# Expert rows stored unnormalised, gathered whole, turned on TensorE, and scattered by row

## The chip, the cores and the metric

The kernel runs on one core of a Trainium2 chip. The time is device microseconds (us) of one execution. Engines: PE (TensorE matmul; PEld is its weight load), DVE (VectorE), ACT (ScalarE), POOL (GpSimd), SP (SyncE). SP, ACT and POOL issue DMAs, each on a queue of its own (q1, q10, q0 in the profile), served by 16 DMA engines.

## What is computed

Two transformer blocks over 512 tokens with 1024 features (D), in float32. The change lies in the last part of the second block, a mixture of 32 experts of which each token takes two from one group:

```
def hierarchical_moe(h, w_rg, b_rg, w_re, b_re, w_gate, w_up, w_down):
    hf = h.reshape(-1, d)                        # h = rms_norm(x, ffn_norm_g)
    g_prob = softmax(hf @ w_rg + b_rg)           # 4 groups
    g_sel = argmax(g_prob);  g_w = g_prob[g_sel]
    e_in_group = (hf @ w_re + b_re)[g_sel]       # 8 experts of that group
    top_p, top_i = top_k(softmax(e_in_group), 2);  top_p = top_p / sum(top_p)
    combine = one_hot(g_sel * 8 + top_i) * (g_w * top_p)
    for every expert e:
        hid = silu(hf @ w_gate[e]) * (hf @ w_up[e])      # 1024 -> 256
        y += (hid * combine[:, e]) @ w_down[e]           # 256 -> 1024
    return y
```

The result is added to the residual x; a gated per-layer embedding follows (`per_layer`), and then the output is written.

## The kernel before

The residual lives in SBUF as 8 chunks `h[k]` of 128 features x 512 tokens. `mixed` adds the last matmuls of the attention part into it chunk by chunk; `router` (L1766) is interleaved with it: as a chunk is ready, its products with the router's weights (L1789) and its squares (L1794) go to TensorE. `gain` is the identity times the norm's weights.

`route` (L1821) then makes, for 4 blocks of 128 tokens, 64 products with `gain` (L1899), which turn the chunks to rows of tokens and multiply by the norm's weights; ACT copies them with the factor of the rms (`xrow`), and four DMAs of ACT's queue store them in DRAM as `xd`, 512 rows of 4 KB. Beside it DVE computes the choice of experts in an order written by hand (L1903 to 2024): one-hots, and a table by matmul (L1881), which gives `gidx`, the index of the token for every slot. A pair of experts is computed together: 64 slots for each, 128 rows. There are 17 positions (16 pairs, and one for experts that have more than 64 tokens; what exceeds that goes through an `overflow` branch, L2133, not taken here).

For each pair `gather_rows` (L2041) issues four indirect DMAs on POOL's queue; each brings quarter rows of 1 KB to 128 partitions, so that four DVE transposes in blocks of 32x32 (`turn_rows`, L2049; `first_rows`, L2061, for the first pair) give `xe`, features x slots. A slot without a token has an index out of range and moves nothing. Then: `up_products` (L2073) 16 products (the trace has two records for each), with the turn of the pair before (`expert_turn`, L2093) behind the first; ACT's silu and one DVE operation (L2085, `eact`); `expert_down` (L2106) 8 products, also with two records; ACT copies the result to `ys`, and ACT's queue stores all 128 rows into `yd` (512 KB, L1717) for pairs 0 to 13. The last three positions stay in SBUF and are brought to their tokens by products with one-hots (`spread`).

The weights, 6 MB per pair, come in pieces of 1 MB on SP's queue (`run` and the ring, L344) into buffers that products release. So this queue goes on when TensorE has used a buffer.

At the end, `rows_back` (L1745) gathers each token's two rows of `yd` by eight indirect DMAs on POOL's queue; `combine` adds up the spread positions (L1757), adds the two rows of each token on DVE (L1760, the "y adds") and turns them by products with the identity (L1762). Then `per_layer`. A scheduler orders the instructions of each engine outside the part that is written by hand; engines run their instructions in order.

Of the kernel before, what the change touches and what calls it, by code (L numbers as in the profile page):

```python
# [22 lines left out]
P = 128  # L23
T = 512
# [30 lines left out]
NSLOT = NST * P + P  # L55
NGR = 4 * NBL
# [3 lines left out]
def shape_constants():  # L60
# [32 lines left out]
    r[:, 32:64] = 2 * (np.arange(32) % NPR) + np.arange(32) // NPR  # L93
    r[:, 64:72] = np.tile(t[:, None] + P * np.arange(TT) + 1, 2)
    r[:, 72:73] = t[:, None] // 32 - 4
    r[:, 73:74] = t[:, None]
# [47 lines left out]
def layout(I):  # L144
# [57 lines left out]
    gu = gu.reshape(NE, 4, KD, 32, 512).transpose(0, 1, 3, 2, 4).reshape(NE, P, 2, 2048)  # L202
    A["w_eg"] = gu.transpose(0, 2, 1, 3).reshape(2 * NE, P, 2048)
# [187 lines left out]
class Kernel:  # L391
# [144 lines left out]
    def run(self, stop):  # L536
# [27 lines left out]
        self.yd = dp.tile([NSLOT, D], F32, name="yd")  # L564
# [1064 lines left out]
    def experts(self, rp, gain, *logits):  # L1629
# [4 lines left out]
        with ExitStack() as ctx:  # L1634
# [3 lines left out]
            r = dict(  # L1638
                slot=kp.tile([P, 2, TT], I32, name="slot"),
                gidx=kp.tile([P, NGR], I32, name="gidx"),  # L1640
                over=self.over,
                table=kp.tile([P, 2, NBL], F32, name="etable"),
                iota=self.w_rt[:, 0:P],
                rows=self.w_rt[:, P:2 * P].rearrange("p (a n) -> p a n", a=2),
                quarter=kp.tile([P, 1], F32, name="quarter"),
            )
            turns = ExitStack()
            tp = turns.enter_context(self.pool("eturn", side="right"))
            xv = xd.rearrange("t (q c) -> (t q) c", q=4)
            gath = [[gain[:, 2 * i:2 * i + 2].rearrange("p a b -> p (a b)") for i in range(4)]]  # L1650
            xe, hid, turned, pairs, begun = {}, {}, {}, [], []

            def first():
                xe[0] = tp.tile([P, KD, P], F32, name="xe")
                yield from self.first_rows(xe[0], gath[0], r["gidx"][:, 0:4], xv)
                begun.extend(self.up_products(xe[0], ring))
                yield begun[-1][1]
            with ExitStack() as c2:
                self.route(c2, tp, xd, r, first(), gain, *logits)
            with ExitStack() as c2:  # L1660
# [606 lines left out]
```

## Time and profile before

| | us |
|---|---|
| median of three runs | 2211.03 (2206.07 to 2212.96) |
| the profiled execution | 2210.73 |
| its span | 2209.0 |
| PE busy | 2081.9 |
| DVE busy | 1069.6 |
| ACT busy | 788.2 |
| POOL busy | 346.7 |

The shares are averages: PE is busy 94% of the whole span, and the experts' part (about 1812 to 2131 us) has other limits. Rows of the timelines give the start, the length and the count of a group of like instructions, and in brackets how long the engine had been idle and what released it.

### The profile page before, as it was taken

Reading aid. Unit: us, or ns where it says so; the run is one execution under the profiler, and the core shown is the slowest. Engines: PE = TensorE matmul, PEld = TensorE weight load, DVE = VectorE, ACT = ScalarE, POOL = GpSimd, SP = SyncE. Lnnn points to the kernel's source line nnn. Section 1 sums busy time; section 2 is a strip of 40 time slices with the busy share of each in tenths; the row PEclk is TensorE's granted clock in tenths of the full one; section 3 lists DMA queues with packets and bytes.
Section 4 is the critical chain, followed back from the end, with each engine's and each line's share of the span. In section 5 each row is a group of like instructions: output and inputs, shape, how many; then the busy total and the mean of one; then the engine's idle time right before and its main releaser. Section 6 shows DMA issues by size and latency. Waiting matters only on the chain. (4 is left out here: it accounts for less than half of the span.)

```text
span 2209.0 us, 25845 instructions
## 1 busy us (share of the span) xinstructions
PE 2081.9 (94%) x10170; PEld 1616.3 (73%) x10170; DVE 1069.6 (48%) x1973; ACT 788.2 (36%) x1186; POOL 346.7 (16%) x444
## 2 busy tenths in 40 slices
PE   7999999999999999999999999999999995977597
PEld 5677788888889878888788888888878882322166
DVE  7887644344476563554554344446654423101136
ACT  4676433122357432333432222343443221111133
POOL 3222200000113111221200000120111114322113
PEclk9999999999999999999999999999999997999899
DMA  5122322322225200110122222322202466999941
GB/s 179 63 78 77 124 96 96 105 96 95 77 70 182 70 33 15 50 47 20 42 93 99 102 96 96 103 98 96 90 29 96 171 251 228 413 416 417 393 161 39
DMA packets 67588, 281.50 MB, mean 127 GB/s; under 512 B 8784, under 2 KB 10104, under 8 KB 54788
## 3 DMA queue, kind: packets, MB, share of 16 engines
q1 hardware_dynamic: 59300, 260.43, 32.2%
q0 software_dynamic: 4560, 8.94, 1.2%
q10 hardware_dynamic: 3600, 10.41, 1.2%
q8 instruction: 82, 1.34, 0.2%
q14 instruction: 46, 0.38, 0.1%
HBM read 272.40 MB, written 12.06 MB: 129 GB/s over the span
## 5 line engine op out<-in xcount | busy, mean ns | idle before, releaser
L275 ACT ACTIVATE whi<-raw 128x1024 fp32r<-128x1024 f32 (+2 forms) x249 | 261.2, 1054 | 647.4 <-PE bank L420 575.5
L420 PE MATMUL bank<-xh,whi 128*128 128x512 f32 x1160 | 464.2, 400 | 9.2 <-ACT xh L430 7.8
L420 PE MATMUL bank<-xh,wlo 128*128 128x512 f32 x1160 | 458.7, 396 | 14.7 <-DVE wlo L276 14.7
L420 PE MATMUL bank<-xl,whi 128*128 128x512 f32 x1160 | 455.5, 393 | 0.0
L276 DVE TENSOR_TENSOR wlo<-raw,whi 128x1024 fp32r<-128x1024 f32 (+2 forms) x249 | 309.5, 1247 | 191.8 <-ACT whi L275 191.6
L420 PEld LDWEIGHTS bank<-xh,wlo 128*128 128x128 f32 x1160 | 220.1, 190 | 67.4 <-DVE wlo L276 16.9
L420 PEld LDWEIGHTS bank<-xh,whi 128*128 128x128 f32 x1160 | 220.4, 190 | 56.3 <-ACT xh L430 7.8
L420 PEld LDWEIGHTS bank<-xl,whi 128*128 128x128 f32 x1160 | 220.0, 190 | 49.7 <-issue 1.2
L447 POOL TENSOR_TENSOR ssq<-ssq,sq 128x512 f32<-128x512 f32 x27 | 39.2, 1453 | 757.0 <-ACT sq L434 757.0
L2073 PE MATMUL bank<-rawa,xe 128*64 128x512 f32 x328 | 103.5, 662 | 40.1 <-DMA rawa<-w_eg 20.3
L420 PE MATMUL bank<-hidh,whi 128*128 128x512 f32 x352 | 137.1, 389 | 0.0
L420 PE MATMUL bank<-hidh,wlo 128*128 128x512 f32 x352 | 137.0, 389 | 0.0
L420 PE MATMUL bank<-hidl,whi 128*128 128x512 f32 x352 | 137.0, 389 | 0.0
L2073 PEld LDWEIGHTS bank<-rawa,xe 128*64 128x64 f32 x328 | 30.2, 150 | 99.0 <-issue 57.7
L434 ACT ACTIVATE prob<-bank 128x512 f32<-128x512 f32 (+1 forms) x96 | 57.1, 595 | 111.1 <-PE bank L1234 81.3
L818 DVE TENSOR_TENSOR fb<-bank,rows 128x512 f32<-128x512 f32 x44 | 30.4, 691 | 133.2 <-PE bank L420 133.2
L1217 PEld LDWEIGHTS acc<-v,prob 128*128 128x128 f32 x640 | 79.8, 192 | 6.2 <-POOL prob L1244 2.3
L1217 PE MATMUL acc<-v,prob 128*128 128x96 f32 x640 | 82.2, 275 | 1.4 <-POOL prob L1244 1.4
L420 PEld LDWEIGHTS bank<-hidh,wlo 128*128 128x128 f32 x352 | 66.1, 188 | 13.8
L420 PEld LDWEIGHTS bank<-hidl,whi 128*128 128x128 f32 x352 | 66.1, 188 | 13.8
L420 PEld LDWEIGHTS bank<-hidh,whi 128*128 128x128 f32 x352 | 66.1, 188 | 13.7
L815 DVE TENSOR_TENSOR fa<-bank,rows 128x512 f32<-128x512 f32 x44 | 30.4, 690 | 88.5 <-PE bank L420 88.5
(571 smaller groups left out, 3710.7 us busy)
## 6 DMA issues: line engine op xcount, KB each, us to landing
raw<-w_gu SPq DMA_DIRECT2D x44, 1024.0 KB, 4.8
rawa<-w_eg SPq DMA_DIRECT2D x41, 1024.0 KB, 14.2
raw<-w_dn SPq DMA_DIRECT2D x20, 1024.0 KB, 4.8
rawa<-w_ed SPq DMA_DIRECT2D x17, 1024.0 KB, 17.1
raw<-w_eg SPq DMA_DIRECT2D x13, 1024.0 KB, 16.4
raw<-w_mix SPq DMA_DIRECT2D x12, 1024.0 KB, 4.8
rawb<-w_eg SPq DMA_DIRECT2D x9, 1024.0 KB, 17.7
yd<-ys ACTq DMA_DIRECT2D x14, 512.0 KB, 8.2
```

The lines of the kernel that those rows point to most:

```text
L275: nc.scalar.activation(hi, r, AF.Copy)
L276: nc.vector.tensor_tensor(lo, r, hi.bitcast(F32), op=ALU.subtract)
L420: i = nc.tensor.matmul(o, a, b, start=first and n == 0, stop=last and n == N - 1)
L434: return self.nc.scalar.activation(o, i, f, **kw)
L447: self.nc.gpsimd.tensor_tensor(self.ssq, self.ssq, sq, op=ALU.add)
L815: nc.vector.tensor_tensor(a, og, rbc, op=ALU.mult)
L818: nc.vector.tensor_tensor(b, ov, rbc, op=ALU.mult)
L1217: i = nc.tensor.matmul(a[:, h * AW:h * AW + AW], e[:K, h * P:h * P + P], v, start=first and h == 0, stop=last and h == HPG - 1)
L2073: last = nc.tensor.matmul(o[s], xe[:, 4 * pi + k, s], w(k), start=pi == 0 and k == 0, stop=pi == 1 and k == 3)
```

## The change

- `router` has a new step `rows(k)`: as a chunk of the residual is ready, four transposes on TensorE, one ACT copy and one DMA of ACT's queue store its features, raw, into `xd` (256 KB, runs of 512 bytes). The 64 products with `gain` and the ACT copies with the rms are gone; the rms now enters in the silu's factor and in the weight (`table` has a third row of numbers), and the norm's weights are multiplied in as rows are turned.
- `gidx` has two entries for each slot: the token, from which to gather, and the assignment (0 to 1023), to which to scatter. One table of 8 matmuls gives both for the 16 pairs; a second gives the factors; a third (`more`) serves the seventeenth position and the overflow.
- `gather_rows` is one indirect DMA of whole rows of 4 KB. Its two buffers are there from the beginning, and pairs 0 and 1 are fetched at once.
- `turn_rows` is eight transposes on TensorE and two DVE multiplications from PSUM.
- The results of pairs 0 to 13 are scattered by row with an indirect DMA of POOL's queue to `yd`, which now has a row for every assignment and is zeroed wholly (4 MB) at the place where 512 KB were.
- The rows back are four plain DMAs of 1 MB on SP's queue, behind the weights; the y adds are ordered behind the last down product.

```diff
+    A["w_eg"] = gu.reshape(NE, 2, 4, P, 512).transpose(0, 1, 3, 2, 4).reshape(2 * NE, P, 2048)
...
-        self.yd = dp.tile([NSLOT, D], F32, name="yd")
+        self.yd = dp.tile([2 * T, D], F32, name="yd")
...
-            nc.gpsimd.dma_start(self.yd[P * NST:P * NST + P, :], z)
+            nc.gpsimd.dma_start(self.yd.rearrange("(n p) d -> p n d", p=P), z.unsqueeze(1).to_broadcast([P, 2 * TT, D]))
...
+            table = kp.tile([P, 3, NBL], F32, name="etable")
+            gidx = kp.tile([P, 2, NBL], I32, name="gidx")
+            r = dict(gidx=gidx, over=self.over, table=table, iota=self.w_rt[:, 0:P])
             turns = ExitStack()
             tp = turns.enter_context(self.pool("eturn", side="right"))
-            xv = xd.rearrange("t (q c) -> (t q) c", q=4)
-            gath = [[gain[:, 2 * i:2 * i + 2].rearrange("p a b -> p (a b)") for i in range(4)]]
             xe, hid, turned, pairs, begun = {}, {}, {}, [], []
-
-            def first():
-                xe[0] = tp.tile([P, KD, P], F32, name="xe")
-                yield from self.first_rows(xe[0], gath[0], r["gidx"][:, 0:4], xv)
+            gath = [tp.tile([P, D], F32, name=f"gath{i}") for i in range(2)]
...
+            for x in gath:
+                nc.gpsimd.memset(x, 0.0)
+
+            def fetch(i):
+                self.gather_rows(gath[i % 2], gidx[:, 0, i:i + 1], xd)
+
+            def rows(i):
+                x = xe[i] = tp.tile([P, KD, P], F32, name=f"xe{i % 2}")
+                return self.turn_rows(x, gath[i % 2])
+
+            def start():
+
+                with self.tc.high_priority():
+                    fetch(0)
+                    fetch(1)
+                yield
+                run(rows(0))
+                yield
                 begun.extend(self.up_products(xe[0], ring))
-                yield begun[-1][1]
+                run(rows(1))
...
-                gath.append([wk.tile([P, 256], F32, name=f"gath{i}") for i in range(4)])
-                for x in gath[1]:
-                    nc.gpsimd.memset(x, 0.0)
...
+                    if between is not None:
+                        run(between)
+                fetch(2)
...
-                        if i + 1 < NPOS:
-                            xe[i + 1] = self.turn_rows((wk, tp)[i % 2], gath[(i + 1) % 2])
-                            if i + 2 < NPOS:
-                                self.gather_rows(gath[i % 2], r["gidx"][:, 4 * i + 8:4 * i + 12], xv)
-                        act = self.expert_up(begun if i == 0 else self.up_products(xe.pop(i), ring), r["table"][:, 1, i:i + 1],
-                                             turn if i else None)
+                        between = rows(i + 1) if 0 < i < NPOS - 1 else None
+                        act = self.expert_up(begun if i == 0 else self.up_products(xe.pop(i), ring), table[:, :, i], turn if i else None)
+                        if 0 < i < NPOS - 2:
+                            fetch(i + 2)
...
-                        y = [self.rows_back(taken[tt], r["slot"], yd, tt) for tt in range(TT)]
+                        y = []
+                        for tt in range(TT):
+                            y.append(taken[tt].rearrange("p (a d) -> p a d", a=2))
+                            nc.sync.dma_start(y[tt], yd.rearrange("(a t p) d -> t p a d", a=2, t=TT)[tt])
...
-                            ys = wk.tile([P, D], F32, name="ys")
+                            ys = rp.tile([P, D], F32, name="ys", tag="xst")
                             self.expert_rows(acc, [ys[:, 512 * n:512 * n + 512] for n in range(2)])
-                            nc.scalar.dma_start(yd[P * (i - 1):P * i, :], ys)
+                            nc.gpsimd.indirect_dma_start(
+                                out=yd, out_offset=bass.IndirectOffsetOnAxis(ap=gidx[:, 1, i - 1:i], axis=0), in_=ys, in_offset=None,
+                                bounds_check=2 * T - 1, oob_is_err=False)
...
-    def rows_back(self, yp, slot, yd, tt):
-
-        y = yp.rearrange("p (a d) -> p a d", a=2)
-        for i in range(2):
-            self.nc.gpsimd.indirect_dma_start(
-                out=y[:, i, :], out_offset=None, in_=yd, in_offset=bass.IndirectOffsetOnAxis(ap=slot[:, i, tt:tt + 1], axis=0),
-                bounds_check=NSLOT - 1, oob_is_err=False)
-        return y
...
+            with self.tc.issue_after(downed.ins):
+                nc.vector.tensor_tensor(z, z, y[tt][:, 1], op=ALU.add)
...
+        def rows(k):
+
+            x = self.bank()
+            for tt in range(TT):
+                nc.tensor.transpose(x[:, P * tt:P * tt + P], self.h[k][:, P * tt:P * tt + P], self.ident)
+            self.act(st[:, k % 2].rearrange("p a b -> p (a b)"), x, AF.Copy)
+            nc.scalar.dma_start(xv[:, :, P * k:P * k + P], st[:, k % 2])
...
+        rows(KD - 1)
...
-            xr = rows2[:, tt % 3 - 1] if tt % 3 else tp.tile([P, D], F32, name="xrow", tag="xe")
-            for hf in range(2):
-                o = self.bank()
-                for i in range(4):
-                    k = 4 * hf + i
-                    nc.tensor.matmul(o[:, P * i:P * i + P], self.h[k][:, P * tt:P * tt + P], gain[:, k, :], start=True, stop=True)
-                self.act(xr[:, 512 * hf:512 * hf + 512], o, AF.Copy, scale=rcol[:, tt:tt + 1])
-            nc.scalar.dma_start(xd[P * tt:P * tt + P, :], xr)
...
-            halves(lambda s: self.act(a[:, s], oh32[:, s].unsqueeze(2).to_broadcast([P, TT, 4, 32]), AF.Copy), n)
-            so = [P, 2 * TT, 4 * NPR]
-            tt_(b, rc[:, 80:80 + 4 * NPR].unsqueeze(1).to_broadcast(so), gr.unsqueeze(2).to_broadcast(so), op=ALU.is_equal)
-            t1 = table(b, 4 * NPR)
-            nc.vector.tensor_copy(out["quarter"], rc[:, 72:73])
-            found = rows(out["gidx"][:, 0:4 * NPR], t1, 4 * NPR)
...
+            halves(lambda s: onehot(at16[:, s], P, row[:, s]), n)
+            o = by_slot(lambda i: at16[:, i], dest, 2 * NPR)
+            places(out["gidx"][:, :, 0:NPR], o, NPR)
+            next(start)
...
+            for i, x in enumerate((rf, w)):
+                tt_(wb[:, :, i], own, x.unsqueeze(2).to_broadcast(so), op=ALU.mult)
+            o = by_slot(lambda i: at[i // TT][:, i % TT], wb, 2 * NPR)
+            next(start)
...
+            onehot(more[:, :, 3], 1 + OB, blk)
+            for i, x in enumerate((rf, w, rc[:, 64:72], rc[:, 72:80])):
+                tt_(more[:, :, i], more[:, :, 3], x.unsqueeze(2).to_broadcast(so), op=ALU.mult)
+            o = by_slot(lambda i: at[i // TT][:, i % TT], more, 4 * (1 + OB))
+            n = 1 + OB
+            nc.vector.tensor_copy(table[:, :, NPR:], o[:, :3 * n].rearrange("p (a n) -> p a n", a=3))
+            places(out["gidx"][:, :, NPR:], o[:, 2 * n:], n)
...
-    def turn_rows(self, pool, gath):
-
-        x = pool.tile([P, KD, P], F32, name="xe")
-        for i in range(4):
-            self.nc.vector.transpose(x[:, :, 32 * i:32 * i + 32], gath[i])
-        return x
...
+    def gather_rows(self, gath, idx, xd):
+
+        self.nc.gpsimd.indirect_dma_start(
+            out=gath, out_offset=None, in_=xd, in_offset=bass.IndirectOffsetOnAxis(ap=idx, axis=0), bounds_check=T - 1, oob_is_err=False)
+
+    def turn_rows(self, x, gath):
+
+        g = self.vec("ffn")
+        for hf in range(2):
+            o = self.bank()
+            for k in range(4):
+                self.nc.tensor.transpose(o[:, P * k:P * k + P], gath[:, 512 * hf + P * k:512 * hf + P * k + P], self.ident)
+            s = slice(4 * hf, 4 * hf + 4)
+            self.nc.vector.tensor_tensor(x[:, s], o.rearrange("p (k s) -> p k s", k=4), g[:, s].unsqueeze(2).to_broadcast([P, 4, P]), op=ALU.mult)
+            yield
...
+        self.hidden = self.act(a, o[:, 0:256], AF.Silu, scale=scales[:, 0:1])
+        nc.vector.scalar_tensor_tensor(a, a, scales[:, 1:2], o[:, 256:512], op0=ALU.mult, op1=ALU.mult)
```

On PE, around the first pairs (the matmuls at L2073 before and L2037 after are the up products; `xe_14505` and `xe_14540` are the turned rows of pairs 0 and 1, `gath_14346` and `gath_14347` their gathered rows). Before, at the end of pair 0's products:

```order
L2073 MATMUL bank<-rawa_13930,xe 64x512
L2073 MATMUL bank<-rawa_13931,xe 64x512
L2000 MATMUL bank<-wb,at_14319 128x48 x4
L2000 MATMUL bank<-wb,at_14320 128x48 x4
L1881 LDWEIGHTS Aoh
L1881 MATMUL bank<-Boh,Aoh 128x32
...
L2073 MATMUL bank<-rawa_13932,xe 64x512
L2073 MATMUL bank<-rawa_13933,xe 64x512
```

After, ahead of pair 0's products and behind them:

```order
L1863 MATMUL bank<-wb,at_14473 128x32 x4
L1863 MATMUL bank<-wb,at_14474 128x32 x4
L2023 MATMUL bank<-ident,gath_14346 128x128 x8
L2037 MATMUL bank<-rawa_13928,xe_14505 64x512
...
L2037 MATMUL bank<-rawa_13931,xe_14505 64x512
L2023 MATMUL bank<-ident,gath_14347 128x128 x8
L1863 MATMUL bank<-more,at_14579 128x32 x4
L1863 MATMUL bank<-more,at_14580 128x32 x4
L2037 MATMUL bank<-rawa_13932,xe_14540 64x512
```

The transposes of rows came to PE, ahead of pair 0's behind the table of factors (`wb`), ahead of pair 1's products with the third table (`more`) between.

On DVE, at the end of the experts (`eact` is the operation behind ACT's silu, for pairs 15 and 16 the last two; L1760 are the y adds; L276 before and L272 after split a weight, L428 and L424 a result). Before:

```order
L428 TENSOR_TENSOR halves<-pT,halves 128x512 x2
L1760 TENSOR_TENSOR rawa_13933<-rawa_13933 128x1024
L1760 TENSOR_TENSOR rawa_13934<-rawa_13934 128x1024
L2085 SCALAR_TENSOR_TENSOR eact<-eact,etable,bank 128x256
L276 TENSOR_TENSOR wlo<-raw,whi 128x1024 x2
L1760 TENSOR_TENSOR rawa_13935<-rawa_13935 128x1024
L1760 TENSOR_TENSOR raw<-raw 128x1024
L428 TENSOR_TENSOR ys_15555<-bank,ys_15555 128x512 x2
```

After:

```order
L2049 SCALAR_TENSOR_TENSOR eact<-eact,etable,bank 128x256
L272 TENSOR_TENSOR wlo<-raw,whi 128x1024 x2
L424 TENSOR_TENSOR ys_15549<-bank,ys_15548 128x512 x2
L2049 SCALAR_TENSOR_TENSOR eact<-eact,etable,bank 128x256
L424 TENSOR_TENSOR ys_15610<-bank,ys_15609 128x512 x2
L1760 TENSOR_TENSOR rawa_13933<-rawa_13933 128x1024
L1760 TENSOR_TENSOR rawa_13934<-rawa_13934 128x1024
L424 TENSOR_TENSOR ys_15733<-bank,ys_15732 128x512 x2
L1760 TENSOR_TENSOR rawa_13935<-rawa_13935 128x1024
```

The y adds moved from ahead of the last two `eact` to behind them; three of them stand ahead of the overflow's branch (which begins with TENSOR_LOAD over), the fourth behind it.

## Rows read from the trace of the kernel before

**Rows 1.** The page's slices of the span: busy tenths of PE, and of DMA.

```profile
PE   7999999999999999999999999999999995977597
...
DMA  5122322322225200110122222322202466999941
```

**Rows 2.** Stretches: start:end, length, busy us of PE PEld DVE ACT POOL, PEclk, DMA share, GB/s.

```profile
1795.00:1812.00 17.00, 17.00 (x92) 14.39 (x91) 1.46 (x3) 2.84 (x5) 2.57 (x2) 1.00 0.04 10
...
1868.00:2083.00 215.00, 177.95 (x736) 57.58 (x736) 29.22 (x84) 31.73 (x63) 50.07 (x51) 0.98 1.01 410
...
2083.00:2098.00 15.00, 0.12 (x1) 0.00 (x0) 2.59 (x3) 0.60 (x1) 5.76 (x6) 0.68 0.97 371
```

**Rows 3.** PE, start of the experts: start, length, line, op, count [idle before <-releaser].

```profile
1814.90 6.05 PE L1899 MATMUL bank<-gain,h 128*128 128x128 f32 x52
...
1826.63 0.92 PE L1881 MATMUL bank<-Boh,Aoh 128*128 128x64 f16 x8 [5.10 <-ACT Aoh L434]
...
1841.10 9.57 PE L2073 MATMUL bank<-rawa,xe 128*64 128x512 f32 x30 [2.78 <-DVE xe L2061]
...
1860.90 7.08 PE L2073 MATMUL bank<-rawa,xe 128*64 128x512 f32 x16 [8.12 <-DVE xe L2049]
...
1867.91 0.44 PE L2093 MATMUL bank<-ident,eact 128*128 128x128 f32 x2
...
1868.28 3.65 PE L2073 MATMUL bank<-rawa,xe 128*64 128x512 f32 x16
```

**Rows 4.** The same view of DVE (two), ACT (two) and POOL (two), start of the experts.

```profile
1824.73 0.69 DVE L1949 TENSOR_TENSOR Boh<-c_route,gr 128x512 f16<-128x512 f32 x1
...
1828.03 0.23 DVE L1888 TENSOR_TENSOR gidx<-w_rt 128x64 int32<-128x64 f32 x1
...
1824.79 0.69 ACT L434 ACTIVATE xrow<-bank,rcol 128x512 f32<-128x512 f32 x1 [4.89 <-DMA xd<-xrow]
...
1826.09 0.33 ACTq L1901 DMA_DIRECT2D xd<-xrow  x1
...
1831.62 1.11 POOL L2041 DMA_INDIRECT gain<-xd,gidx  x1 [10.29 <-DVE cm L1975]
...
1853.72 1.08 POOL L1666 MEMSET gath<- 128x256 f32 x4
```

**Rows 5.** DMA 1870 to 2083 us: queues (packets, MB, share); issues (KB, us to landing).

```profile
q10 hardware_dynamic: 2304, 7.87, 9.1%
...
q0 software_dynamic: 2349, 2.36, 3.5%
...
yd<-ys ACTq DMA_DIRECT2D x14, 512.0 KB, 8.2
...
gain<-xd,gidx POOLq DMA_INDIRECT x24, 6.3
```

**Rows 6.** Timeline of PE at the end of the experts.

```profile
2098.31 0.69 PE L2093 MATMUL bank<-ident,eact 128*128 128x128 f32 x2 [15.19 <-DVE eact L2085]
...
2098.93 4.80 PE L2073 MATMUL bank<-rawa,xe 128*64 128x512 f32 x13
...
2131.11 11.33 PE L1757 MATMUL bank<-spread,ys 128*128 128x512 f32 x48 [2.09 <-DVEq L2133]
```

**Rows 7.** Timeline of DVE at the end of the experts.

```profile
2091.62 1.23 DVE L1760 TENSOR_TENSOR rawa<-rawa 128x1024 f32<-128x1024 f32 x1 [20.27 <-DMA rawa<-yd,slot]
...
2097.77 0.48 DVE L2085 SCALAR_TENSOR_TENSOR eact<-eact,etable,bank 128x256 f32<-128x256 f32 x1
```

**Rows 8.** DMA 2076 to 2100 us: a queue; an issue with us to landing.

```profile
q0 software_dynamic: 1133, 4.14, 45.6%
...
rawa<-yd,slot POOLq DMA_INDIRECT x6, 12.5
```

**Rows 9.** Timelines of POOL and ACT around the zeroing of yd.

```profile
263.36 0.76 POOL L572 DMA_DIRECT2D yd<-z  x1 [0.31 <-POOL z L571]
...
290.31 1.19 ACT L427 ACTIVATE hidh<-fa 128x512 fp32r<-128x512 f32 x2 [0.61 <-DVE fa L819]
```

More of the change, by code (lines that the diff above doesn't have):

```diff
@@ L1720, in experts @@
                 assert W.ld == len(W.order)
-                self.overflow(wk, tp, gath, r, xv)
-                sums = self.combine(pairs, y)
+                downed = self.downed
+                self.overflow(wk, tp, r)
+                sums = self.combine(pairs, y, downed)
             turns.close()
@@ L1934, in route @@
             pick(ex, rc[:, 32:64].unsqueeze(1).to_broadcast(sh))
[L1935 to L1936 removed]
+            nc.vector.tensor_reduce(up, Ef[:, :, NPR:], AX.X, ALU.add)
+            so = [P, 2 * TT, NPR]
+            onehot(own, NPR, ex)
+            for i in range(2):
+                nc.gpsimd.tensor_tensor(dest[:, :, i], own, rc[:, 64 + 8 * i:72 + 8 * i].unsqueeze(2).to_broadcast(so), op=ALU.mult)
@@ new lines, in route @@
+            stt(row, up, float(CAP), pos, op0=ALU.mult, op1=ALU.add)
+            tt_(row, row, q, op=ALU.add)
+            halves(lambda s: onehot(at16[:, s], P, row[:, s]), n)
+            o = by_slot(lambda i: at16[:, i], dest, 2 * NPR)
+            places(out["gidx"][:, :, 0:NPR], o, NPR)
+            next(start)
+            table = out["table"]
+            self.act(table[:, 2, 0:NPR], o[:, 0:NPR], AF.Copy)
+            at = [self.stat.tile([P, TT, P], F32, name=f"at{i}", tag=("sq", "rbc")[i]) for i in range(2)]
@@ L1996, in rest @@
-            begun = next(first)
-            with self.tc.issue_after(begun.ins):
-                o = self.bank()
-                for i in range(2 * TT):
-                    nc.tensor.matmul(o[:, :2 * NBL], at[i // TT][:, i % TT], wb[:, i].rearrange("p a b -> p (a b)"), start=i == 0, stop=i == 2 * TT - 1)
-            by_slot = o[:, :2 * NBL]
-            nc.vector.tensor_copy(out["table"].rearrange("p a b -> p (a b)"), by_slot)
-            stt(bs, bs, 2.0, g2, op0=ALU.mult, op1=ALU.add)
-            ts(away, ov, -1e3, 998.0, ALU.mult, ALU.add)
@@ L2006, in rest @@
-            tt_(gr, bs, away, op=ALU.add)
-            so = [P, 2 * TT, 2 * NEX]
-            bo = b[:, :, 0:2 * NEX]
-            tt_(bo, rc[:, 80:80 + 2 * NEX].unsqueeze(1).to_broadcast(so), gr.unsqueeze(2).to_broadcast(so), op=ALU.is_equal)
-            with self.tc.issue_after(begun.ins):
-                t2 = table(bo, 2 * NEX)
-            rows(out["gidx"][:, 4 * NPR:4 * NBL], t2, 2 * NEX)
-            ts(sl, sl, float(P * NST), None, ALU.min)
-            nc.vector.tensor_copy(out["slot"].rearrange("p a t -> p (a t)"), sl)
@@ L2017, in rest @@
-            ovf, inb = small("ovf", [1 + NEX]), small("inb", [NEX, NE])
+            ts(ov, q, 1.0, -1e4, ALU.is_lt, ALU.mult)
+            stt(pos, bs, float(CAP), pos, op0=ALU.mult, op1=ALU.add)
+            ts(pos, pos, -float(CAP), None, ALU.add)
+            floor_div(blk, pos, P)
+            stt(row, blk, -float(P), pos, op0=ALU.mult, op1=ALU.add)
+            tt_(row, row, ov, op=ALU.add)
+            at = [self.stat.tile([P, TT, P], F32, name=f"at{i}", tag=("sq", "rbc")[i]) for i in range(2)]
@@ L2075, in up_products, with expert_up @@
             yield o, last
-    def expert_up(self, steps, weight, between=None):
+    def expert_up(self, steps, scales, between=None):
         nc = self.nc
```

189 lines of the change are left out of this document (67 added, 122 removed).

## The prediction

> **What bounds the kernel now.** I read the page's slices first: TensorE is at 9 tenths for most of the span, but it falls to 5 in slice 34, 7 in 36 and 37 and 5 in 38, while the DMA row stands at 9 in 35 to 38 [rows 1]. A slice is 55 us, so that these are the experts. The stretches by time say the same: from 1868 to 2083 us the DMA engines are busy the whole time, at 410 GB/s, while PE is busy 177.95 of 215 us; from 2083 to 2098 PE does 0.12 us of work [rows 2]. So the experts have three parts, each with its own bound: a start (about 1812 to 1868), bound by a chain through routing, gathers and turns; a middle, bound by the transfer of 6 MB of weights per pair; an end, in which PE first stands still and then works off what is left. Ahead of 1812 PE itself is the bound: 17.00 busy of 17 us [rows 2]. Behind the combining matmuls (2131.11) the change touches nothing, so that what the combine gains, the program gains.
>
> **Start, the chain.** In the timeline of PE [rows 3], the 52 products of the row writing take 6.05 us, 0.116 us each; the table of indices starts at 1826.63 after a wait for the one-hot on ACT; the first pair's products run without a break from 1841.10; the second pair's begin at 1860.90 after 8.12 us for the turn of its rows; the middle begins at 1868.28.
>
> *Added.* The transposes of the residual (4 for each of 8 chunks) stand between the products of the rising residual, which PE bounds. 28 lie ahead of the last chunk's: at 0.116 each, products of the same shape in one run [rows 3], 3.3 us; at 0.185 each, as the two turns of 128x128 at 1867.91 that reach to 1868.28 [rows 3], 5.2 us. I take 3.7, nearer the first, since these too come in runs of four. The eight ACT copies and eight stores of 256 KB lie beside it: ACT is busy 2.84 of these 17 us and the DMA share is 0.04 [rows 2].
>
> *Removed and shortened.* Before, the one-hot stood behind an xrow copy on ACT that itself waited 4.89 us for a store [rows 4]; the new one-hots are made on DVE, with fewer steps ahead, so I put the indices about 1.7 us earlier in the chain than 1828.26. The first gather before began at 1831.62, 3.4 us behind the indices: the last store of rows was issued only at 1826.09 and the gather needs it landed [rows 4]. In the changed kernel that store goes out behind the last transposes, some 9 us earlier, and the gather no longer waits. Instead of four gathers 1.3 us apart and four DVE turns, the last of them after another 2.78 us of PE's wait [rows 3], there is one gather, 8 PE transposes (8 x 0.116 to 0.185, about 1.2 us) and two multiplies of 128x512 (0.69 us as the one-hot of that size [rows 4]). But the matmuls for the weight table now stand ahead of these transposes on PE. By the small steps of 0.1 to 0.3 us between dependent DVE operations they end near 1831.5, and the gather lands about then. Two more us give 1833.6 in the old clock, plus 3.7 is 1837.3, against 1841.10: **3.8 us gained**. Bounds: 1 us (transposes at 0.185 and a landing of 4 us) to 6 us (both terms favourable).
>
> *Pair 1.* The 8.12 us hole came from clearing the second buffer and gathering only after the routing pool had closed (memset at 1853.72) [rows 4]. Now both gathers go out at once. In its place a new wait: on DVE some 30 small operations for the overflow table stand behind the multiplies of pair 1, about 6.2 us, and on PE the eight matmuls of that table stand ahead of pair 1's products. Turn, multiply, chain and table make about 10 us between the pairs; before it was 10.2, from 1841.10 + 9.57 to 1860.90 [rows 3]. So I count nothing here, and the 3.8 us are carried to the middle.
>
> **Middle, the transfers.** Of the DMA time from 1870 to 2083, the queue of ACT took 9.1% for 7.87 MB and the gathers' queue 3.5% for 2.36 MB [rows 5]. Before, all 128 slot rows of a pair are written, 14 x 0.524 = 7.34 MB. But 512 tokens with two experts each are 1024 rows of 4 KB, 4.19 MB, in all 17 positions together; so a scatter of filled rows moves at least 3.15 MB less, at 410 GB/s [rows 2] 7.7 us. The gathers' 3.5% of 213 us, 7.5 us, is above 2.36 MB at that rate, 5.8 us: whole rows of 4 KB instead of quarters save up to 1.7 us. Together 9.4 us if the saving falls on all DMA engines alike, some 11 with the rows of the last three positions, which aren't scattered; nothing if the fullest engine moves as much as before. I take **7 us**, nearer the upper end, since q10's time is in proportion to its bytes (9.1% of 213 us is 19.4, 7.87 MB at 410 GB/s are 19.2), with 0 to 11 as bounds. How filled rows lie over the engines no row here shows. The Trainium skill (DMA: Bandwidth & Descriptors, "The descriptor swizzle") gives the engine by partition, four partitions each and repeating within 32, by which filled rows, first in each half of 64, load the low engines of each half more; an estimate by it alone would put this term nearer 4 us.
>
> PE does not become the bound. A pair takes PE 48 records of products (two for each instruction) at 3.65 us per 16 and the turn [rows 3], 11.3 us, and eight transposes more make it 12.2 to 12.8; the DMA engines need about 215/14 = 15.4 us for it [rows 2], less 0.5. Those 2 us of cover hide the transposes; without it they would cost 14 x 1.2 us. DVE, busy 29.22 of 215 us there [rows 2], has room for two multiplies instead of four turns.
>
> **End.** The row to read is the turn of pair 15 on PE at 2098.31, idle 15.19 us for eact [rows 6]. On DVE, eact ran at 2097.77, right behind the y adds, the first of which had waited 20.27 us for the rows back [rows 7]. eact's inputs were there at about 2083. In the changed kernel the y adds stand behind both last eact (the order on DVE), and the rows back are four plain loads behind the last weights on SP, so that their 4.14 MB no longer run beside the weights between 2076 and 2100 [rows 8]. From the turn to the combine took 2131.11 - 2098.31 = 32.8 us [rows 6], of which about 1.8 us were a cold TensorE (13 records took 4.80 us at 2098.93 [rows 6], against 3.65 for 16 [rows 3]). New in it: the weights of the last two down products (4 MB = 10 us, released only as the up products go) cost perhaps 2 us of wait; the third y add (1.23 us) stands ahead of the branch on DVE for which PE waits. So from 2083 it is 32.8 - 1.8 + 2 + 1.2 = 34 us to the combine, against 32.8 + 15.2 = 48: **14 us gained**, bounds 8 (the rows back, 10 us behind 10 us of weights, end the chain) and 16. The loads of the gate's weights move behind the branch; the products that use them stand on PE behind the combine's 48 (11.33 us [rows 6]) and 64 smaller ones, and 4 MB take 10 us: nothing.
>
> **Elsewhere.** The zeroing grows from 512 KB to 4 MB at 263.36, and by the program only the next hidh copy on ACT, at 290.31, waits for it [rows 9]; 10 us of transfer end by about 280, so nothing, and at most some 5 us if weights are delayed behind it.
>
> **Sum.** 3.8 + 7 + 14 = 24.8 us off the profiled execution, 2210.73 (its span 2209.0; the median of the runs is 2211.03, the same within 0.02%): **2186 us**. By the ends of the terms: 1 + 0 + 8 = 9, and 6 + 11 + 16 = 33.
>
> **Rivals.** (A) The transfers give nothing: scattered rows keep the fullest DMA engine as busy as whole writes did, and the y loads end the chain. 3.8 + 0 + 10 gives 2197. For it: the rows don't show that the saving falls on the fullest engine. Against: q10's bytes nearly halve [rows 5].
> (B) The start is lost, because transposes between other products don't overlap as a run of 52 does. The two turns at 1867.91 end after 0.44 us [rows 3], 0.22 each; the 30 records of the first pair took 9.57 us where 16 take 3.65 later [rows 3], 1.4 times as long, because the granted clock there was nearer to the lower of its levels (1.2 GHz). At 0.22 x 1.4 = 0.3 us, 28 transposes take 8.4 us in place of 3.7: the start loses 0.9 instead of gaining 3.8: 2191. Against: the 52 products at 0.116, and a PE that is busy all the time ahead of 1812 [rows 2, 3]. The Trainium skill (TensorE: Matmul & The Clock Gate, Part 4) puts a transpose in transpose mode at about 275 ns in a kernel and says that it does not count as busy for the clock; an estimate by that figure is 28 x 0.275 = 7.7 us, and the start would give nothing.
> (C) Slower. POOL's queue is in order and now alternates gather and scatter; each scatter waits for ACT's copy of its pair and for the scatter before it, and the next gather stands behind. A gather then has about one pair's period, 15 us, for the scatter ahead of it and its own landing. Before, a store of all rows landed in 8.2 us [rows 5], and only the scatter's issue (about 1 us) counts if the scatter before has landed. From the point at which a scatter needs more than some 15 us to land, every us more is paid in 14 pairs: at 17 us, 28 us, 2186 + 28 = 2214; at 18, 2228. Rows read by index under full load took 12.5 us [rows 8], which is under it, as is the gathers' 6.3 [rows 5].
> (D) The change doesn't do what it says at the end: PE still waits at the last pairs, for y or weights, as long as before. 3.8 + 7 + 2 gives 2198.
>
> **How the numbers follow.** Forecast 0.60 (2179 to 2194), A 0.14, B 0.10, D 0.07, C 0.06, and 0.03 that it comes out within the bound of no change. A difference of 0.3%, some 6.6 us, is about what a measurement can tell from none. Faster: 0.60 + 0.14 + 0.10 + 0.07 = 0.91; same 0.03; slower 0.06. The range holds the forecast, A, B and D with the ends of the terms: 2174 to 2202.
>
> **What would show it.** Right: PE's first expert products at about 1837 and the middle from about 1864; q10 nearly empty in the middle and q0 at 5 to 6 MB; no idle of 15 us on PE ahead of the turn of pair 15, y adds behind eact. Wrong: a row-writing transpose above 0.2 us a piece, L2023 waiting for gathers in every pair, the middle still 215 us long, or the combine waiting for the y loads.

## The result and the profile after

| | before | after |
|---|---|---|
| median, us | 2211.34 (2206.07 to 2212.96) | 2187.27 (2186.09 to 2188.93) |
| span of the profiled execution, us | 2209.0 | 2184.4 |
| PE busy, us | 2081.9 | 2094.6 |

The ratio is 0.9896, with a 95% interval of 0.9878 to 0.9914: 24 us faster, where 2186 us were forecast. PE is busy for longer and the program is shorter, so the gain came from waits. The slices of the page after, PE and DMA, to be read against [rows 1]:

```profile
PE   7999999999999999999999999999999996998897
...
DMA  5122432222224310111122322232212285899961
```

PE's 7, 7 and 5 in slices 36 to 38 are now 9, 8 and 8; what is left is the 6 in slice 34, the start.

**The start.** PE's timeline (start, length, line, tile shapes, count, idle before and releaser), and POOL's first gather:

```profile
1816.31 0.61 PE L1800 MATMUL bank<-ident,h 128*128 128x128 f32 x4
...
1831.83 3.60 PE L1863 MATMUL bank<-wb,at 128*128 128x32 f32 x16 [3.92 <-DVE wb L1968]
1835.24 1.95 PE L2023 MATMUL bank<-ident,gath 128*128 128x128 f32 x8
1837.12 8.07 PE L2037 MATMUL bank<-rawa,xe 128*64 128x512 f32 x32
1845.12 1.09 PE L2023 MATMUL bank<-ident,gath 128*128 128x128 f32 x8
1853.26 3.60 PE L1863 MATMUL bank<-more,at 128*128 128x32 f32 x16 [7.05 <-DVE more L1997]
1856.79 5.04 PE L2037 MATMUL bank<-rawa,xe 128*64 128x512 f32 x16
1861.76 0.44 PE L2057 MATMUL bank<-ident,eact 128*128 128x128 f32 x2
```
```profile
1829.23 1.12 POOL L2014 DMA_INDIRECT gath<-xd,gidx  x1 [3.47 <-DVE rr L1959]
```

The first pair's products begin at 1837.12 instead of 1841.10 [rows 3]; the first turn (L2057, before L2093) comes at 1861.76 instead of 1867.91. The hole between the two pairs is still there, with another cause: PE waits 7.05 us for `more` (the third table, for the overflow), then spends 3.60 on it. The stretches, in the columns of [rows 2], show what DMA did meanwhile:

```profile
1841.00:1847.00 6.00, 5.21 (x28) 1.98 (x24) 1.19 (x2) 0.00 (x0) 0.52 (x1) 1.00 0.68 257
1847.00:1853.00 6.00, 0.00 (x0) 0.00 (x0) 5.42 (x26) 0.00 (x0) 0.47 (x1) 0.70 1.01 422
1853.00:1857.00 4.00, 3.74 (x18) 3.71 (x20) 0.22 (x3) 0.00 (x0) 0.00 (x0) 0.50 0.35 145
1857.00:1862.00 5.00, 5.00 (x18) 1.46 (x17) 2.64 (x10) 1.76 (x2) 0.00 (x0) 0.74 0.00 0
```

From 1847 to 1853 PE does nothing and DVE is busy 5.42 of 6 us; DMA runs out of free buffers and stands still from 1857 to 1862.

**The middle.** The queues from 1864 to 2068 us (packets, MB, share), and the scatter with its us to landing:

```profile
q1 hardware_dynamic: 10529, 75.79, 90.4%
q0 software_dynamic: 3869, 6.39, 8.3%
q10 hardware_dynamic: 288, 0.52, 0.7%
...
yd<-ys,gidx POOLq DMA_INDIRECT x14, 8.4
```

ACT's queue is nearly empty; scatters and gathers together are 6.39 MB in these 204 us, where stores and gathers were 10.2 in 213 us [rows 5].

**The end.** PE's turn of pair 15 and its combine, then DVE, then SP:

```profile
2073.36 0.44 PE L2057 MATMUL bank<-ident,eact 128*128 128x128 f32 x2
...
2074.70 3.22 PE L2037 MATMUL bank<-rawa,xe 128*64 128x512 f32 x13 [0.90 <-DMA rawa<-w_eg]
...
2079.95 0.64 PE L2037 MATMUL bank<-rawa,xe 128*64 128x512 f32 x1 [1.41 <-DMA rawa<-w_eg]
...
2106.57 11.35 PE L1756 MATMUL bank<-spread,ys 128*128 128x512 f32 x48 [2.73 <-DVEq L2097]
```
```profile
2084.14 0.48 DVE L2049 SCALAR_TENSOR_TENSOR eact<-eact,etable,bank 128x256 f32<-128x256 f32 x1 [9.36 <-ACT eact L430]
...
2094.81 1.96 DVE L1760 TENSOR_TENSOR rawa<-rawa 128x1024 f32<-128x1024 f32 x1 [3.18 <-DMA rawa<-yd]
```
```profile
2084.01 2.71 SPq L1712 DMA_DIRECT2D rawa<-yd  x3
```

PE no longer waits for eact, and the y adds stand behind the last one. The turn row is the mark for the stages: the first turn ends the start, the turn of pair 15 ends the middle (before it would have stood at 2098.31 - 15.19 = 2083.12 [rows 6]), the first product of the combine ends the end.

| stage, to its mark | before | after | gain | forecast |
|---|---|---|---|---|
| start, to the first turn | 1867.91 | 1861.76 | 6.15 | 3.8 |
| middle, to the turn of pair 15 | 215.2 | 211.6 | 3.6 | 7 |
| end, to the combine | 48.0 | 33.2 | 14.8 | 14 |
| together | | | 24.55 | 24.8 |

The sum is right to 0.3 us, but two of its terms were off by 2.4 and 3.4 us in opposite directions. The experiments are on these.

### The profile page after: what moved, and what is told of

It reads as the page before. It is cut to its first block, busy times and chain, and to the rows that moved or that the text cites. A ratio compares the mean times of both kernels' runs of the same rounds, so it can differ in the third digit from the quotient of the medians.

```text
span 2184.4 us, 25894 instructions
## 1 busy us (share of the span) xinstructions
PE 2094.6 (96%) x10282; PEld 1631.2 (75%) x10282; DVE 1070.8 (49%) x1926; ACT 789.4 (36%) x1187; POOL 299.8 (14%) x394
## 3 DMA queue, kind: packets, MB, share of 16 engines
q1 hardware_dynamic: 60388, 264.63, 33.2%
q0 software_dynamic: 5504, 12.30, 1.5%
## 5 line engine op out<-in xcount | busy, mean ns | idle before, releaser
L272 DVE TENSOR_TENSOR wlo<-raw,whi 128x1024 fp32r<-128x1024 f32 (+2 forms) x249 | 309.1, 1245 | 196.0 <-ACT whi L271 195.7
L2037 PE MATMUL bank<-rawa,xe 128*64 128x512 f32 x328 | 93.3, 619 | 11.8 <-DMA rawa<-w_eg 11.5
L2037 PEld LDWEIGHTS bank<-rawa,xe 128*64 128x64 f32 x328 | 27.0, 142 | 61.2 <-issue 41.3
```

The source lines that it names most:

```text
L272: nc.vector.tensor_tensor(lo, r, hi.bitcast(F32), op=ALU.subtract)
L2037: last = nc.tensor.matmul(o[s], xe[:, 4 * pi + k, s], w(k), start=pi == 0 and k == 0, stop=pi == 1 and k == 3)
```

## The experiments

Each ratio is to the kernel before, in the same series of runs, with a 95% interval. The third column is the time from the first turn to that of pair 15, in each kernel's one profiled execution.

| kernel | ratio | middle, us | from the turn of pair 15 to the combine, us |
|---|---|---|---|
| before | 1 | 215.2 | 48.0 |
| changed | 0.9896 (0.9878 to 0.9914) | 211.6 | 33.2 |
| before, y adds behind eact (e1) | 0.9964 (0.9951 to 0.9977) | 214.5 | 39.3 |
| changed, slots laid evenly (e2) | 0.9880 (0.9866 to 0.9895) | 207.7 | 33.2 |
| changed, overflow table earlier (e3) | 0.9868 (0.9853 to 0.9883) | 211.4 | 33.4 |
| changed, all rows scattered (e4) | 0.9925 (0.9912 to 0.9938) | 216.4 | 33.5 |
| e2 and e3 together (e5) | 0.9842 (0.9829 to 0.9856) | 206.5 | 33.9 |
| e5, table of factors behind pair 0 (e6) | 0.9882 (0.9866 to 0.9897) | 207.7 | 33.1 |
| changed, scatter of one pair only (e7) | 0.9846 (0.9833 to 0.9860) | 199.8 | 34.1 |
| changed, row transposes twice (e8) | 0.9919 (0.9906 to 0.9933) | 213.1 | 33.0 |
| e2 and e4 together (e9) | 0.9917 (0.9904 to 0.9931) | 213.2 | 32.9 |

**e1: the order of the y adds, alone, in the kernel before.**

```diff
-            nc.vector.tensor_tensor(z, z, y[tt][:, 1], op=ALU.add)
+            with self.tc.issue_after(acted.ins):
+                nc.vector.tensor_tensor(z, z, y[tt][:, 1], op=ALU.add)
...
+        self.acted = nc.vector.scalar_tensor_tensor(a, a, weight, o[:, 256:512], op0=ALU.mult, op1=ALU.mult)
```

> The kernel before with one thing changed: the four y adds are ordered on DVE behind the last eact; the eight gathers of rows back stay on POOL's queue where they were. Theory 1 (the end's gain has two causes, the order of the y adds and the 4.14 MB that the gathers put beside the weights): PE's idle of 15.2 us ahead of the turn of pair 15 goes, but the up products of pair 16 still wait for weights that land at about 2092 and 2095, so that the combine comes 7 to 9 us earlier: about 2203 us. Rival (the order alone is all of it): about 2196.5. Rival (the loads alone are all of it): 2211, as before.

Measured: 2202.23 us, 7.4 less than before in its series. PE at the end:

```profile
2081.75 0.44 PE L2095 MATMUL bank<-ident,eact 128*128 128x128 f32 x2
...
2083.10 3.65 PE L2075 MATMUL bank<-rawa,xe 128*64 128x512 f32 x14 [0.91 <-DMA rawa<-w_eg]
...
2089.30 1.07 PE L2075 MATMUL bank<-raw,xe 128*64 128x512 f32 x2 [2.56 <-DMA raw<-w_eg]
...
2093.16 1.11 PE L2075 MATMUL bank<-rawa,xe 128*64 128x512 f32 x1 [2.79 <-DMA rawa<-w_eg]
```

The wait of 15.19 us is gone, and waits for the weights of pair 16 took part of its place, since the gathers of rows back still ran beside them (3.15 MB of queue q0 between 2076 and 2100). The order is worth 48.0 - 39.3 = 8.7 us of the end. The other 6.1 (39.3 to 33.2) are what is left to the changed kernel, where the loads stand on SP behind the weights. No run has these loads alone, but the rows say where the 6.1 lie, in the products of pair 16: their waits for weights are 6.3 us here (0.91, 2.56 and 2.79) and 2.3 there (0.90 and 1.41), and behind the last wait here the granted clock was 0.51 (2093.0 to 2097.5), with the products 0.86 us apart instead of 0.43. So both causes of Theory 1 are there. The line of the change that names the last down product is not what moved the adds: built without it, the program has the same instructions in the same order on every engine. That they moved because they now wait for loads that are issued late is likely, but no run shows it.

**e2: the filled rows laid evenly.**

```diff
+    r[:, 240:368] = (t & 64) | (t & 32) | ((t & 3) << 3) | ((t >> 2) & 7)
...
+            at = 240 if n == P else 80
+            return tt_(out, rc[:, at:at + n].unsqueeze(1).to_broadcast(out.shape), x.unsqueeze(2).to_broadcast(out.shape), op=ALU.is_equal)
```

> The changed kernel with the slots of an expert laid over the 64 partitions in another order, so that the filled ones lie evenly over groups of four partitions instead of first; everything else alike. Theory 1 (the middle gained only 3.6 us because the filled rows fall on few DMA engines and the fullest sets the pace): the middle from the first to the last turn shortens by 4 to 6 us, 2182 to 2183 us. Rival (the saving is lost at the end of the middle, where the ring of buffers is small and DMA engines idle for some 4 us, whatever lies on which engine): within 1 us of the changed kernel, 2187.

Measured: 2182.29 us. First and last turn of the middle:

```profile
1859.96 0.44 PE L2059 MATMUL bank<-ident,eact 128*128 128x128 f32 x2
...
2067.70 0.44 PE L2059 MATMUL bank<-ident,eact 128*128 128x128 f32 x2
```

The middle is 3.9 us shorter with the same bytes, instructions and queues. The intervals of the two ratios overlap at their ends (0.9895 and 0.9878), so the time alone would leave it weak; the stage says where it is. So where the filled rows lie matters. The Trainium skill (DMA: Bandwidth & Descriptors, "The descriptor swizzle") gives, for a full transfer to 128 partitions, the engine that writes each partition; that a transfer with rows left out follows the same rule no row shows.

The traces do show that the DMA engines drift apart. For each load of 1 MB a trace holds sixteen landing times, as many as there are engines, though not which is whose. From the first to the last of the sixteen it takes some 2 us for the loads that land from 1864 to 1900 (medians of 1.7 to 2.2). For those from 2020 to 2050, in the kernels of this run and of runs further down, it takes:

| kernel | gathers' rows | scatter's or store's rows | first to last landing, us (median) |
|---|---|---|---|
| before | first in each half | all | 7.6 |
| changed | first in each half | first in each half | 15.4 |
| e4 | first in each half | all | 9.6 |
| e7 | first in each half | one pair only | 9.0 |
| e2 | evenly | evenly | 6.9 |
| e9 | evenly | all | 3.5 |

A load counts as landed with the last of its sixteen parts, so the engine that lags most sets the pace, and the even layout takes more than half of the drift away. The idle time of the rival is there too, in the changed kernel's stretches:

```profile
2055.00:2060.00 5.00, 4.14 (x17) 1.24 (x16) 0.00 (x0) 0.00 (x0) 0.00 (x0) 1.00 0.47 162
...
2070.00:2075.00 5.00, 4.10 (x18) 1.37 (x16) 1.38 (x2) 1.47 (x3) 0.00 (x0) 1.00 0.60 216
```

Shares of 0.47 and 0.60 leave some 4.7 us idle. But it is not the same whatever lies on which engine: with the even layout, stretches of 5 us at the same place in the work leave 2.4 (shares of 0.88 and 0.65).

**e3: the overflow table's operations beside pair 0's products.**

```diff
                 begun.extend(self.up_products(xe[0], ring))
+                yield
                 run(rows(1))
...
+            next(start)
             o = by_slot(lambda i: at[i // TT][:, i % TT], more, 4 * (1 + OB))
```

> The changed kernel with the DVE operations of the overflow table put ahead of the multiplies of pair 1's rows, so that they run beside pair 0's products, and that table's matmuls on PE behind pair 1's transposes; everything else alike. Theory 1 (the 7.05 us that PE waits between pair 0 and pair 1 are the whole of that chain, and the DMA engines, idle from about 1853 to 1863, get them back): pair 1 begins at about 1849.5 instead of 1856.8, 2180 us. Rival (the middle is bound by transfers that were already under way, and gives the time back): at most 2 us, 2185 or more.

Measured: 2180.10 us. PE between the pairs, and the stretches from 1850 on:

```profile
1845.61 1.09 PE L2025 MATMUL bank<-ident,gath 128*128 128x128 f32 x8
1846.54 1.87 PE L1864 MATMUL bank<-more,at 128*128 128x32 f32 x16
1848.34 5.37 PE L2039 MATMUL bank<-rawa,xe 128*64 128x512 f32 x22
1853.63 0.44 PE L2059 MATMUL bank<-ident,eact 128*128 128x128 f32 x2
```
```profile
1850.00:1856.00 6.00, 6.00 (x32) 2.55 (x30) 2.55 (x7) 2.14 (x3) 0.78 (x1) 1.00 1.03 388
1856.00:1862.00 6.00, 6.00 (x30) 2.01 (x28) 0.48 (x1) 1.67 (x3) 0.20 (x1) 1.00 0.98 396
```

The hole has gone, the DMA engines no longer stand still, and the first turn comes 8.1 us earlier, all of which reaches the combine (2098.41 against 2106.57); between the medians it is 7.2 us, by the ratios 6.2. So the new wait that the prediction named was worth nearly as much as the 8.12 us [rows 3] that the change removed, and it stood there only because DVE's order put these operations behind the multiplies of pair 1.

**e4: all rows scattered.**

```diff
+            ts(dump, rc[:, 64:65], float(2 * T - 1), None, ALU.add)
+            tt_(out["dst"], out["gidx"][:, 1, 0:NPR], dump.to_broadcast([P, NPR]), op=ALU.min)
```

> The changed kernel with every one of the 128 rows of a pair scattered, the unfilled ones to rows that nobody reads: the same queue and instructions, 7.34 MB instead of the filled part. Theory 1 (the bytes of the scatter count in the middle): 3.4 MB more at 2.44 us per MB is 8 us if they fall evenly, 4 to 5 if the engines that held the filled rows set the pace: 2191 to 2195. Rival (the middle doesn't depend on the scatter's bytes): 2187 to 2188.

Measured: 2193.29 us. Queue q0 from 1864 to 2068 us, then in the whole run of this kernel and of the changed one:

```profile
q0 software_dynamic: 3744, 9.32, 11.6%
...
q0 software_dynamic: 5504, 15.74, 1.9%
...
q0 software_dynamic: 5504, 12.30, 1.5%
```

9.32 MB instead of 6.39 within that stretch, which ends before this kernel's middle does; 3.44 MB more in the whole run. The middle is 4.8 us longer (216.4): the filled rows' saving, but 4.8 instead of the 7.7 that the prediction counted for it. With all rows stored, as before the change, the middle is also 1.2 us longer than before (215.2): of the up to 1.7 us counted for gathering whole rows nothing shows.

**e7: nearly no scatter.**

```diff
+                            if i == 1:
+                                nc.gpsimd.indirect_dma_start(
```

> The changed kernel with the scatter of the first pair alone; the results of pairs 1 to 13 are left out, and nothing is stored for them. Theory (in the middle the fullest DMA engine sets the pace): storing all rows took 19.2 us of DMA time in the kernel before, and of these the filled rows saved only 4.8, so the scatter still costs up to 13 us there: 2174 to 2177. Rival (bytes count evenly): 9 us at most, 2178 to 2180. Second rival (the end of the middle is bound by the ring of buffers): 2183 or more.

Measured: 2175.45 us; queue q0 in the same stretch and in the whole run:

```profile
q0 software_dynamic: 2016, 2.89, 3.9%
...
q0 software_dynamic: 3632, 8.79, 1.1%
```

The middle is 11.8 us shorter than in the changed kernel, for 3.51 MB less on this queue in the whole run (12.30 - 8.79): 3.4 us per MB, where 2.44 were counted. The unfilled rows of e4 cost 4.8 us for 3.44 MB more (15.74 - 12.30), 1.4 us per MB. So the filled rows are dear and the unfilled ones cheap, which bytes alone don't explain; a fullest engine does, and the drift in the table of e2 fits it (9.0 us without the scatters, 15.4 with the filled rows, 9.6 with all rows).

**e9: is it the scatter's rows or the gathers'?** The two edits of e2 and e4 together.

> All 128 rows of a pair scattered, and the slots laid evenly over the partitions: the two edits together, so that the scatter is even in both layouts and only the gathers' rows change places. Theory 1 (the even layout helped the scatter alone): as with all rows in the old layout, a ratio to the kernel before of 0.991 to 0.994. Theory 2 (it helped the gathers alone): 4 us less than that, 0.989 to 0.9915, and the middle from the first to the last turn at about 212.5 instead of 216.4 us. Half of each would show a middle of about 214.4.

Measured: 2189.14 us, ratio 0.9917; the middle 213.2 us, 3.2 less than with all rows in the old layout, between the 212.5 of the second theory and the 214.4 of the third. By the ratio it would be less (0.9917 against 0.9925, 1.8 us, within the intervals). So the gathers gain from the even layout, and their drift falls from 9.6 to 3.5 us (table of e2); how much of the 3.9 us is theirs is not settled. Within the even layout the unfilled rows still cost only 5.5 us (213.2 - 207.7) for the same 3.44 MB, 1.6 us per MB, so the layout is not all that makes them cheap; the rest is open.

**e8: the transposes of rows twice.**

```diff
-                self.nc.tensor.transpose(o[:, P * k:P * k + P], gath[:, 512 * hf + P * k:512 * hf + P * k + P], self.ident)
+                for _ in range(2):
+                    self.nc.tensor.transpose(o[:, P * k:P * k + P], gath[:, 512 * hf + P * k:512 * hf + P * k + P], self.ident)
```

> The changed kernel with every transpose of gathered rows issued twice, the second over the first: 8 more on PE per pair, about 0.9 us each pair, nothing else. Theory (the middle is bound by transfers and PE's share is hidden): the first pairs take 12.6 instead of 11.7 us, but the last turn comes at most 1 us later; with the two at the start some 2 us in all: 2188 to 2190. Rival (PE bounds the pairs): 0.9 us x 14 = 12 us, 2199.

Measured: 2191.25 us. The first turn came at 1865.64, the second at 1878.20, 12.56 us apart (11.69 in the changed kernel); the middle was 1.5 us longer, not 12. PE's transposes are hidden in the middle, nearly: while the ring still holds weights that were loaded ahead, PE sets the pace, and the DMA engines, busy all the while, give most of it back later. The time is 1.3 us above the range of the theory, and in the profiled execution 5.1 us above the changed kernel's. Besides the 1.5 us of the middle, 2.6 us lie in the two turns of the start (3.65 and 1.97 us instead of 1.95 and 1.09), and the routing was reached 1.4 us later in that execution, ahead of the edit.

**e5 and e6: a version that beats both.** e5 has the edits of e2 and e3.

> The changed kernel with both edits, the slots laid evenly over the partitions and the overflow table's operations ahead of pair 1's multiplies. Theory (one is worth about 5 us in the middle, the other about 7 at the start, and they touch different stages): they add up, 12 us under the changed kernel, 2175. Rival (a start that comes earlier meets a middle that is then bound by something else, PE or the ring of buffers): 2178 or more.

Measured: 2174.56 us, ratio 0.9842: 12.7 us under the changed kernel's median, about as much as the two apart (5.0 and 7.2). These medians are of different series; by the ratios it is 11.9 us against 3.5 and 6.2, with intervals of some 3 us each way. The stages add up: the first turn is 7.5 us earlier and the middle 5.1 shorter. In e6 the products of the table of factors stand behind pair 0's:

```diff
-            o = by_slot(lambda i: at[i // TT][:, i % TT], wb, 2 * NPR)
             next(start)
-            nc.vector.tensor_copy(table[:, 0:2, 0:NPR], o.rearrange("p (a n) -> p a n", a=2))
             next(start)
+            o = by_slot(lambda i: at[i // TT][:, i % TT], wb, 2 * NPR)
+            nc.vector.tensor_copy(table[:, 0:2, 0:NPR], o.rearrange("p (a n) -> p a n", a=2))
```

> As the kernel with both edits, and the eight matmuls of the table of factors behind pair 0's products on PE instead of ahead of the first transposes. Theory (the first gather lands at about 1834.5 and holds the transposes anyway, and the 1.8 us of matmuls then stand between pair 0 and pair 1): within 1.5 us of that kernel, 2174 to 2176. Rival (the 3.6 us of these matmuls ahead of the first transposes are lost time): 3 us less, 2172.

Measured: 2183.31 us, 8.8 slower than e5, which neither theory had. PE and one row of DVE:

```profile
1825.11 0.19 PE L1922 MATMUL bank<-M,tri 128*128 128x32 bf16 x1 [6.04 <-DVE M L1917]
...
1835.04 1.94 PE L2027 MATMUL bank<-ident,gath 128*128 128x128 f32 x8 [5.76 <-DMA gath<-xd,gidx]
1836.91 8.84 PE L2041 MATMUL bank<-rawa,xe 128*64 128x512 f32 x32
1845.69 1.97 PE L1866 MATMUL bank<-wb,at 128*128 128x32 f32 x16
1847.49 1.07 PE L2027 MATMUL bank<-ident,gath 128*128 128x128 f32 x8
1854.02 3.60 PE L1866 MATMUL bank<-more,at 128*128 128x32 f32 x16 [5.46 <-DVE more L2000]
```
```profile
1847.69 0.19 DVE L1975 COPY etable<-bank 128x32 f32<-128x32 f32 x1 [9.99 <-PE bank L1866]
```

The same PE rows in e5:

```profile
1825.34 0.19 PE L1922 MATMUL bank<-M,tri 128*128 128x32 bf16 x1 [6.05 <-DVE M L1917]
...
1836.83 1.95 PE L2027 MATMUL bank<-ident,gath 128*128 128x128 f32 x8
```

The first part was right in kind: the transposes now wait for the gather until 1835.04. Counted from the routing's first matmuls (1825.34 in e5, 1825.11 here) they begin 9.93 us later instead of 11.49, so that the 3.60 us of `wb` ahead of them had cost 1.6 us. But the copy of the table on DVE, 0.19 us, waited 9.99 us for the moved products, and the whole chain of the overflow table stood behind it; the hole that e3 had closed was back. It is the same mechanism once more, now of the edit's own making: one instruction that waits holds an engine's queue.

## Why the prediction was right, and where its steps were not

The mechanisms that the prediction named were there in all three stages. That its sum came within 0.3 us is in part luck: the start gave 2.35 us more than counted and the middle 3.4 less. The rows for the first point, of the changed kernel and then of the kernel before:

```profile
1791.57 1.00 PE L1789 MATMUL bank<-w_rt,h 128*128 128x64 f32 x8
1792.41 0.61 PE L1800 MATMUL bank<-ident,h 128*128 128x128 f32 x4
...
1798.45 1.00 PE L1789 MATMUL bank<-w_rt,h 128*128 128x64 f32 x8
```
```profile
1790.40 1.00 PE L1789 MATMUL bank<-w_rt,h 128*128 128x64 f32 x8
...
1796.90 1.00 PE L1789 MATMUL bank<-w_rt,h 128*128 128x64 f32 x8
```

- **Transposes in the residual.** Two groups of logits (L1789) follow each other 0.38 us later than before (1791.57 to 1798.45, against 1790.40 to 1796.90), so that four transposes cost 0.38 us, 28 of them 2.7 us; 3.7 were taken. Rival B fell: 0.095 us a piece, below even the 0.116 of [rows 3], and the granted clock stayed at its upper level there. The Trainium skill's 275 ns in one kernel (TensorE: Matmul & The Clock Gate, Part 4) is not what runs of four or eight show here; there a piece takes 0.10 to 0.14 us at the upper level of the clock (1.09 us for eight) and 0.24 at the lower (1.95).
- **Indices and gather.** The indices were written at 1828.18 (2.5 us earlier in the chain once the 2.7 us of transposes are taken off, 1.7 forecast), the first gather began at 1829.23, no longer held by the stores. The first products came at 1837.12, forecast 1837.3. Two errors cancel there: the transposes in the residual cost 1.0 us less than counted, and the chain to the end of the matmuls of `wb` (1831.83 + 3.60 = 1835.43) took some 1.2 us more.
- **The start's term, 3.8 against 6.15.** Its mechanism and the first products were right. What failed is "I count nothing here" for pair 1: the hole was 11.6 us (1845.19 to 1856.79) instead of 10.2, but both pairs' products ran faster, 8.07 us for 32 records instead of 9.57 for 30, and 5.04 for 16 instead of 7.08 [rows 3]: 1.4 us lost, 1.5 and 2.0 gained. From 1841 to 1847 the granted clock was 1.00, its upper level (2.4 GHz); before it was 0.57, near the lower (1.2 GHz). Ahead of it PE had been busy 6.00 us of the 6 from 1832 to 1838, with the table, the transposes and the first products; before it had been busy 2.73 of the 15 from 1826 to 1841. The runs vary it: behind 1.9 us of unbroken work on PE (e6) the first 32 records took 8.84 us, behind 5.3 (changed) 8.07, behind 7.0 (e8) 7.13. The prediction carried the old durations over without asking what PE does before them.
- **The middle's term, 7 against 3.6.** The mis-sized step is the saving of the scatter: it was taken by bytes (7.7 us and up) and measured 4.8 (e4), and 5.5 in the even layout (e9 to e2). From the 4.8 go 1.2 us by which the middle with all rows stored is longer than before; there the up to 1.7 us for whole gathered rows, which the sum held too, don't show, and what the 1.2 us are was not taken apart. The bound "nothing if the fullest engine moves as much as before" was the right question: the engines' drift grew from 7.6 to 15.4 us (e2). The value near the upper end was the wrong choice, and the 4 us that the estimate by the Trainium skill's swizzle gave were nearer, though its working is not shown.
- **PE in the middle.** Not the bound, as forecast, but for the first six pairs it sets the pace, 11.69 us a pair against 10.82 before (five pairs). e8 shows that most of this comes back.
- **The end's term, 14 against 14.8.** As forecast, from two causes: e1 gives 8.7 us for the order, and 6.1 are left for the loads. The waits for weights were 0.90 and 1.41 us, 2 were counted; the third y add ahead of the branch is there (PE's wait is 2.73 instead of 2.09).
- **The zeroing** took 16.1 us to land, and hidh's copy ran at 289.74 (290.31 before [rows 9]): nothing, as forecast.
- **Rival C** did not come: scatters landed in 8.4 us, well under the 15 from which POOL's order would have cost; PE waited for no gather in the middle. A fell with e4 (the filled rows save 4.8 us), though by half only, since the middle gave 3.6 of 7; D fell with the end's rows.

## What to carry to other kernels

When a wait is removed, look at what stands in order behind it and ahead of the next user on each engine: here a chain that serves a later position took 7 us between the first two pairs, and moving it, with two lines, was worth 6 to 7 us beside the 24 of the whole change. Bytes that are saved in a transfer-bound stage count only as far as the fullest DMA engine is relieved; here laying the filled rows evenly over the partitions cost no instruction and gave 3.9 us. Durations of a stage that begins after idle time can't be carried over to a kernel in which the engine is busy before it.

## What the runs showed of the hardware

- A scatter by row index that skips indices out of range moves only the rows that are in range (12.30 MB on its queue in the whole run against 15.74 with all rows written), and its issue kept POOL about 1.0 us in both cases.
- The same eight products of 128x32 in float32 took 3.60 us at a granted clock of 0.50 (1853 to 1857 in the changed kernel) and 1.87 at 1.00 (e3): behind 7.05 us without work they took nearly twice as long.
- Under loads that keep all DMA engines busy, uneven rows make the sixteen parts of a 1 MB load land ever further apart: 15.4 us from first to last after some 170 us, 3.5 with even rows (e9).
- The first y adds took 1.96 us where the same operation took 1.23 before [rows 7]; POOL and ACT were working then, and the cause was not tried.
